# Three small jobs moved one quarter block later in TensorE's order: the second x half of a state-space group, the copy of the index keys, and the transpose of B in the second layer

## The chip, the cores and the metric

One core of one Trainium2 chip runs the whole program. Its engines are TensorE (PE in the profile: matmuls and transposes; PEld is its weight load), VectorE (DVE), ScalarE (ACT), GpSimd (POOL) and SyncE (SP, which issues nearly all DMAs). The metric is the device time of one execution in microseconds (us); the time of a kernel is the median of its runs.

## The reference, cut to what matters

Two layers work on 272 tokens (16 learned meta tokens and 256 inputs) of width 2048. All branches of a layer take their inputs from one projection, and their outputs go through one output projection:

```
h <- h + RMSNorm_post(W_out [ silu(gA)*PoolMix(vA) | SSD(xBC,z,dt) | silu(gC)*DSA(q,k,v) ])

SSD, for each of 4 groups of 8 heads:  xs, B, C = silu(conv4(xBC));  dt = softplus(.)
    cb = C B^T;   y = (cb * decay) (xs*dt)  +  C * state;   state = B^T (decay * xs*dt)
    y = y + D*xs;  y = RMSNorm_group(y * silu(z))
DSA:  ki = rope(index key);  score[q,s] = sum_h w_h relu(qi_h . ki[s]);  keep the 64 best s of each query
PoolMix:  windowed means of v, minus v, times a 256x256 matrix for each of 4 groups
```

Everything is fp32 in the reference. The second layer's first 16 tokens are needed only as inputs of the others, not as outputs.

## The kernel before

**Precision and weights.** Each weight matrix is cut into blocks of 256 columns, and a block into four quarters of 512 rows. A quarter is loaded in one DMA (`wr`). `split` then makes the two parts that the matmuls use, half a quarter at a time: ScalarE casts to fp32r (`wh`, line 211) and VectorE subtracts for the remainder (`wl`, line 219). `wh` has 10 buffers and `wl` 9, so both engines may run some four quarters ahead of TensorE. A product takes three matmuls (lines 244 to 246); a quarter block is 24 of them.

**Order.** The order of all engines is written out by the Python program, and each engine works strictly in the order in which its instructions are written. TensorE's main stream is the sequence of blocks: iq, k, v, q and ag, then for each group g of the state-space part xs(2g), xs(2g+1), BC(g), z(2g), z(2g+1), then pv and pg (pool), then the output projection. All work behind a block is a generator (`post_xs`, `post_BC`, `post_misc` and others). After each quarter block `tick()` resumes every generator once, in the order in which they were started; what a generator writes up to its next `yield n` stands between two quarter blocks, and `yield n` lets it sleep for n quarters. `yield from until(key)` sleeps in steps of one quarter until another generator has put `key` into `done`. Waits for data are then semaphores on the chip.

**Generators that the change and the prediction speak of.**
- `post_misc` turns the index keys and the dt columns. It writes the rope of the keys (`ikp`, finished on GpSimd, line 452), copies them (`ikh`, lines 478 and 489), multiplies them by a piece of the identity so that they also stand on partitions 0 to 63 (`pik`, line 486, on TensorE) and forms the remainders (`ikl`, line 490 on GpSimd, line 495 on VectorE). The key "ik" lets `post_iq` write the score matmuls `pq` (line 593), which read `ikh` and `ikl`. ScalarE then takes `s` from `pq` (line 598), and VectorE adds it into the scores (lines 605, 607). When all are in, VectorE picks the 64 best, and the attention heads (`pl`, line 674, which reads `qs`, line 763) begin.
- `post_xs(2g+j)` is half j of group g: evacuation, convolution on VectorE (line 802, six instructions), silu and the copy `xr` on ScalarE (lines 806, 826), transposes `px` on TensorE (lines 845, 847), `xdt` on VectorE (852, 855), a product on GpSimd (860), casts `xdd` on ScalarE (864, 865), remainders on VectorE (867, 868), and then the key `xdd{g}_{j}`. Half 0 of group g begins its convolution only after `until(y{g-1})`, that is when the last z half of the group before is written.
- `post_BC(g)` makes the convolution, silu and the copy `br` (886), sleeps `BY` quarters, and turns B (`pb`, 889, 890) and multiplies C by B (`pc`, 894); VectorE then writes `cbm` and the remainders of `bt` (899 to 904). It waits for `xdd{g}_0` and `xdd{g}_1`, sleeps one quarter and writes the state matmuls `pst` (913 to 917). Then it starts the four `decay` generators, whose last step sets `M{g}_{c}`.
- `post_z` waits for `M{g}_{c}`, writes the products of the group (`ssd_y`), and sets `y{g}` at the end of its second half; then it norms the group (`rsqrt_g`, eleven GpSimd instructions, lines 272 to 282) and writes the mix (1015, 562, 563).
- `post_pv(0)` waits for `y3`, makes the window sums on GpSimd (1040, 1042), and then `py_`, `pyh` and `pyl` (1045, 1049, 1052), and sets `ys0`. `pool_mm(0)` stands in TensorE's stream after the second quarter of the block pv1; it calls `tick()` in a loop until `ys0` is there, and then writes the matmuls `ppo` (1068 to 1070), which read `pyh` and `pyl`.

Of the kernel before, what the change touches and what calls it, by code (L numbers as in the profile page):

```python
# [10 lines left out]
F32 = mybir.dt.float32  # L11
F32R = mybir.dt.float32r
AF = mybir.ActivationFunctionType
OP = mybir.AluOpType
# [4 lines left out]
P = 128  # L19
# [71 lines left out]
BY = 1  # L91
# [11 lines left out]
def hybrid(ctx: ExitStack, tc: tile.TileContext, I, out, dbg=None, layers=2):  # L103
# [9 lines left out]
    sm = ctx.enter_context(tc.tile_pool(name="sm", bufs=2))  # L113
# [5 lines left out]
    V, A, G, TE = nc.vector, nc.scalar, nc.gpsimd, nc.tensor  # L119

    def pair(name):
        return pr.tile([P, 2, T], F32, name=name, tag="pair")

    def aux(name):
        return psa.tile([P, 512], F32, name=name, tag="a")

    def rep8(ap):

        return bc(ap[:, None, :], [ap.shape[0], 8, 16])

    def by8(ap):
        return ap.rearrange("p (e s) -> p e s", e=8)

    def dump(name, ap):
        if name in dbg:
            nc.gpsimd.dma_start(dbg[name], ap)

    def bc(ap, shape):
        return ap.to_broadcast(shape)
# [190 lines left out]
    ikh = const.tile([P, T], F32R, name="ikh")  # L330
    ikl = const.tile([P, T], F32R, name="ikl")
# [23 lines left out]
    def layer(L, hs):  # L355
# [11 lines left out]
        def until(key):  # L367
            while key not in done:
                yield 1
# [71 lines left out]
        def rope_v(dst, ps, nch, c0, idx):  # L441

            b = 2 if idx else 0
            n = T - c0
            t = pair("ropet")
            for i, p_ in enumerate(ps if isinstance(ps, list) else [ps[:, :nch]]):
                p_ = p_[:, None, :] if isinstance(ps, list) else p_
                m = p_.shape[1]
                V.stream_shuffle(t[:, i:i + m, c0:T], p_[:, :, c0:T], SHI if idx else SHQ)
                V.tensor_tensor(dst[:, i:i + m, c0:T], p_[:, :, c0:T], bc(rope[:, b:b + 1, c0:T], [P, m, n]), op=OP.mult)  # L450
            G.tensor_tensor(t[:, :nch, c0:T], t[:, :nch, c0:T], bc(rope[:, b + 1:b + 2, c0:T], [P, nch, n]), op=OP.mult)  # L451
            G.tensor_tensor(dst[:, :nch, c0:T], dst[:, :nch, c0:T], t[:, :nch, c0:T], op=OP.add)
# [16 lines left out]
        def post_misc(ps):  # L469
            yield from until("r")  # L470
            ps3 = ps[:, None, :]
            mt = pair("mt")
            V.tensor_tensor(mt[0:64, 0], ps[0:64, :T], r[0:64], op=OP.mult)
            V.tensor_copy(by8(mt[0:48, 1, 0:128]), rep8(mt[0:48, 0, 0:16]))
            ikp = pair("ikp")
            rope_v(ikp, ps3, 1, 0, True)
            yield 1
            A.copy(ikh[64:128], ikp[64:128, 0])
            ptr = aux("ptr")
            pv_ = ptr[:, 0:144].rearrange("p (b c) -> p b c", b=3)  # L480
            TE.transpose(pv_[:, 0], mt[0:48, 1, 0:128], ident[0:48, 0:48])
            for b in (1, 2):
                TE.transpose(pv_[:, b], mt[0:48, 0, TB[b][0]:TB[b][1]], ident[0:48, 0:48])  # L483

            pik = aux("pik")[0:64, 0:T]
            TE.matmul(pik, ident[:, 64:128], ikp[:, 0], start=True, stop=True)
            dx = sm.tile([P, 3, 48], F32, name="dx", tag="dx", bufs=1)
            yield 1
            A.copy(ikh[0:64], pik)
            G.tensor_tensor(ikl[64:128], ikp[64:128, 0], ikh[64:128].bitcast(F32), op=OP.subtract)  # L490
            V.tensor_copy(dx, pv_)
            V.tensor_scalar(iw, dx[:, 1:3, 32:48], 2.0 ** -5, None, op0=OP.mult)
            done.add("iw")
            yield 1
            V.tensor_tensor(ikl[0:64], pik, ikh[0:64].bitcast(F32), op=OP.subtract)
            done.add("ik")
            yield 1
            yield MY

            def st(name):  # L500
                return sm.tile([P, 3, 32], F32, name=name, tag=name, bufs=1)

            h_ = [wk.tile([P, n], F32, name="dtw", tag=tag) for n, tag in ((256, "bt"), (T, "cbm"))]
            n_, w_, z_, z2 = (t[:, o:o + 96].rearrange("p (b h) -> p b h", b=3) for t in h_ for o in (0, 96))
            x_, p_ = st("sx"), st("sp")
            ae = sm.tile([P, 1, 32], F32, name="ae", tag="ae", bufs=1)
            V.tensor_tensor(x_, dx[:, :, 0:32], bc(dtc[:, L, 0:1], [P, 3, 32]), op=OP.add)
            V.scalar_tensor_tensor(n_, x_, -1.0, x_, op0=OP.mult, op1=OP.min)
            A.activation(w_, n_, AF.Exp)
            A.activation(ae[:, 0], dtc[:, L, 1], AF.Exp)  # L510
            yield 1
            V.tensor_scalar(n_, w_, 2.0, None, op0=OP.add)
            V.reciprocal(z_, n_)
            V.tensor_tensor(z_, z_, w_, op=OP.mult)
            V.tensor_tensor(z2, z_, z_, op=OP.mult)
            V.tensor_scalar(p_, z2, 1.0 / 17, None, op0=OP.mult)
            for c in (15, 13, 11):
                V.scalar_tensor_tensor(p_, p_, 1.0 / c, z2, op0=OP.add, op1=OP.mult)
            yield 1
            for c in (9, 7, 5, 3):  # L520
                V.scalar_tensor_tensor(p_, p_, 1.0 / c, z2, op0=OP.add, op1=OP.mult)
            V.scalar_tensor_tensor(p_, p_, 1.0, z_, op0=OP.add, op1=OP.mult)
            V.tensor_scalar(n_, x_, 0.0, None, op0=OP.max)
            V.scalar_tensor_tensor(dt, p_, 2.0, n_, op0=OP.mult, op1=OP.add)
            da = st("sx")
            V.scalar_tensor_tensor(da, dt, -1.0, bc(ae, [P, 3, 32]), op0=OP.mult, op1=OP.mult)
            yield 1
            yield 1

            pcs = aux("pcs")  # L530
            TE.matmul(pcs[:, 0:32], tri8[0:16], da[0:16, 0], start=True, stop=True)
            for b in (1, 2):
                TE.matmul(pcs[:, 32 * b:32 * b + 32], tri, da[:, b], start=True, stop=True)
            for b in range(2):
                n = NB[b]
                TE.matmul(pcs[:, 96 + 32 * b:128 + 32 * b], ones[0:n, :], da[0:n, b], start=True, stop=True)
            pct = aux("pct")
            for b, (s0, s1) in enumerate(TB):
                n = s1 - s0
                TE.matmul(pct[0:32, s0:s1], da[0:n, b], tri[0:n, 0:n], start=True, stop=True)  # L540
            yield 1
            V.tensor_copy(cs, pcs[:, 0:96].rearrange("p (b h) -> p b h", b=3))
            V.tensor_tensor(wd, pcs[:, 96:160].rearrange("p (b h) -> p b h", b=2), cs[:, 0:2], op=OP.subtract)
            A.activation(wd, wd, AF.Exp)
            A.activation(dec, pcs[:, 128:160], AF.Exp)
            cst_ = pr.tile([32, T], F32, name="csT", tag="pair")
            V.tensor_copy(cst_, pct[0:32, :T])
            dump(f"dt{L}", dt.rearrange("p a b -> p (a b)"))
            dump(f"cs{L}", cst_)
            yield 1  # L550
            G.tensor_scalar(wd[:, 0], wd[:, 0], pa[:, MSK:MSK + 1], None, op0=OP.mult)
            A.dma_start(csd, cst_)
            done.add("cs")
# [254 lines left out]
        def post_xs(i, ps):  # L808
# [19 lines left out]
            if j == 0:  # L828
                yield from until("cs")
                if g == 0:  # L830
                    for a_ in range(4):
                        yield from until(f"mixA{a_}")
                s["xdt"] = wk.tile([P, 3, 8, 64], F32, name="xdt", tag="xdt")
                s["xdd"] = wk.tile([P, 3, 512], F32R, name="xdd", tag="xdd")
                s["csb"] = slots.tile([P, 8, T], F32, name="csb", tag=f"S{SP_[0]}")
                nc.sync.dma_start(s["csb"], csd[8 * g:8 * g + 8].rearrange("h t -> (h t)").partition_broadcast(P)
                                    .rearrange("p (h t) -> p h t", h=8))
                s["yg"] = wk.tile([P, 4, T], F32, name="yg", tag="yg")
            else:
                while "yg" not in s:  # L840
                    yield 1
            px = aux("px")
# [28 lines left out]
        def post_BC(g, ps):  # L871
# [12 lines left out]
            br = pair("br")[:, 0, 0:128]  # L884
            bT, cT = x[:, 0], x[:, 1]
            A.copy(by8(br), rep8(bT[:, 0:16]))
            yield BY
            pb = aux("pb")
            TE.transpose(pb[:, 0:P], br, ident)
            TE.transpose(pb[:, P:2 * P], bT[:, 16:144], ident)  # L890
# [202 lines left out]
        def lead_0():  # L1093
# [14 lines left out]
            for hh in range(8):  # L1108
# [10 lines left out]
                if hh == 3:  # L1119
                    early()  # L1120
            spawn(post_misc(pm))
            for b in range(NLEAD):
                spawn(post["iq"](b, lead[b]))

        def lead_1():
# [62 lines left out]
            for hh in range(8):  # L1188
# [8 lines left out]
                if hh > 4:  # L1197
                    tick()
            spawn(post_misc(pm))
            for i in range(2):  # L1200
                spawn(post_iq(i, e[i]))
# [312 lines left out]
```

## Time and profile before

| | us |
|---|---|
| median of three runs | 1584.16 |
| lowest, highest run | 1581.88, 1584.36 |
| the profiled execution: its own time | 1581.26 |
| the profiled execution: its span | 1579.5 |
| TensorE busy in the span | 1540.3 (98%) |
| VectorE, ScalarE, GpSimd busy | 1206.4 (76%), 884.6 (56%), 416.5 (26%) |
| mean granted TensorE clock | 0.997 |

The profiled execution ran 2.9 us faster than the median of the runs, and its time is 1.8 us more than its span. All rows are of this one execution. "Busy" counts the union of an engine's instructions. The number in brackets at the end of a timeline row is the idle time of that engine just before the instruction, with what ended it; a row with "xN" holds N instructions in a row, its second number being the time from the first one's start to the last one's end.

### The profile page before, as it was taken

The numbers are of one execution on the slowest core, as the hardware profiler recorded it, in microseconds if no ns is written. First come the engines' busy times: TensorE is split into PE (matmuls) and PEld (weight loads), VectorE is DVE, ScalarE is ACT, GpSimd is POOL, SyncE is SP. The second block draws the span as 40 slices with busy tenths as digits, with TensorE's granted clock in tenths as the row PEclk, the third lists the DMA queues.
The fourth block names the chain that finished last, engine by engine and source line by source line (L and its number), as shares of the span: only waits on it lengthen the run. The fifth ranks groups of instructions, "written<-read, shape, count | busy, mean of one in ns | idle before, by whom it ended". The sixth has DMA issues, their size and how long they took to land. (4 is left out here: it accounts for less than half of the span.)

```text
span 1579.5 us, 31128 instructions
## 1 busy us (share of the span) xinstructions
PE 1540.3 (98%) x11788; PEld 1475.4 (93%) x11788; DVE 1206.4 (76%) x2217; ACT 884.6 (56%) x1663; POOL 416.5 (26%) x416
## 2 busy tenths in 40 slices
PE   7999999999999999999998999999999999999997
PEld 6899999999999999999998999999999999988886
DVE  7899777798989776545588998787989888764554
ACT  6455566656667444444455555666676565444542
POOL 3823342233342421000103314322333324200000
PEclk9999999999999999999999999999999999999999
DMA  6545445454544465565536454454545455566652
GB/s 232 204 146 174 138 135 180 143 189 136 188 172 154 130 207 169 191 217 176 171 108 230 152 173 157 149 188 148 197 153 181 174 162 164 190 225 207 208 188 93
DMA packets 78310, 272.44 MB, mean 172 GB/s; under 512 B 8848, under 2 KB 11984, under 8 KB 77136
## 3 DMA queue, kind: packets, MB, share of 16 engines
q1 hardware_dynamic: 78064, 270.39, 51.5%
q8 instruction: 92, 1.51, 0.4%
q14 instruction: 58, 0.48, 0.1%
q10 hardware_dynamic: 96, 0.07, 0.0%
HBM read 266.03 MB, written 4.40 MB: 171 GB/s over the span
## 5 line engine op out<-in xcount | busy, mean ns | idle before, releaser
L219 DVE TENSOR_TENSOR wl<-wr,wh 128x512 fp32r<-128x512 f32 (+1 forms) x952 | 712.7, 773 | 270.0 <-PE go L246 70.5
L211 ACT CAST wh<-wr 128x512 fp32r<-128x512 f32 (+1 forms) x952 | 564.6, 615 | 430.2 <-PE go L245 91.7
L244 PE MATMUL g0xs<-u,wh 128*128 128x272 f32 x256 | 74.8, 292 | 0.0
L244 PE MATMUL g1xs<-u,wh 128*128 128x272 f32 x256 | 74.6, 291 | 0.0
L244 PE MATMUL g0z<-u,wh 128*128 128x272 f32 x256 | 74.5, 291 | 0.0
L246 PE MATMUL go<-mixS,wl 128*128 128x272 f32 x256 | 74.1, 290 | 0.0
L246 PE MATMUL g0xs<-u,wl 128*128 128x272 f32 x256 | 74.1, 290 | 0.0
L246 PE MATMUL g0z<-u,wl 128*128 128x272 f32 x256 | 74.1, 290 | 0.0
L246 PE MATMUL g1xs<-u,wl 128*128 128x272 f32 x256 | 74.1, 289 | 0.0
L244 PE MATMUL go<-mixS,wh 128*128 128x272 f32 x256 | 74.0, 289 | 0.0
L245 PE MATMUL g1xs<-u,wh 128*128 128x272 f32 x256 | 73.7, 288 | 0.0
L245 PE MATMUL g0xs<-u,wh 128*128 128x272 f32 x256 | 73.7, 288 | 0.0
L245 PE MATMUL g0z<-u,wh 128*128 128x272 f32 x256 | 73.6, 288 | 0.0
L245 PE MATMUL go<-mixS,wh 128*128 128x272 f32 x256 | 73.6, 288 | 0.0
L244 PE MATMUL g1z<-u,wh 128*128 128x256 f32 x256 | 72.7, 284 | 0.0
L451 POOL TENSOR_TENSOR ropet<-ropet,rope 128x512 f32<-128x512 f32 (+2 forms) x20 | 33.2, 1661 | 147.7 <-PE ptr L483 66.1
L246 PE MATMUL g1z<-u,wl 128*128 128x256 f32 x256 | 71.7, 280 | 0.0
L245 PE MATMUL g1z<-u,wh 128*128 128x256 f32 x256 | 71.6, 280 | 0.0
L948 POOL TENSOR_TENSOR M<-M,cbm 128x512 f32<-128x512 f32 x32 | 45.9, 1434 | 93.4 <-ACT M L941 93.4
L802 DVE SCALAR_TENSOR_TENSOR xs<-xpad,par,xs 128x272 f32<-128x272 f32 x96 | 62.1, 712 | 0.0
L1262 POOL TENSOR_TENSOR acc<-acc,osq 128x544 f32<-128x544 f32 x6 | 8.2, 1370 | 168.8 <-ACT osq L1248 168.8
L266 PE MATMUL got<-wh,mixS 128*128 128x512 f32 x128 | 50.8, 397 | 0.0
(531 smaller groups left out, 5523.9 us busy)
## 6 DMA issues: line engine op xcount, KB each, us to landing
wr<-wi SPq DMA_DIRECT2D x334, 512.0 KB, 3.3
wr<-wo SPq DMA_DIRECT2D x128, 512.0 KB, 3.4
csb<-csd SPq DMA_DIRECT2D x8, 1088.0 KB, 8.4
x<-xT SPq DMA_DIRECT2D x8, 272.0 KB, 5.0
res<-xT SPq DMA_DIRECT2D x4, 544.0 KB, 6.0
h1d<-o SPq DMA_DIRECT2D x4, 544.0 KB, 7.7
wr<-plw SPq DMA_DIRECT2D x8, 256.0 KB, 2.6
hx<-h1d SPq DMA_DIRECT2D x8, 256.0 KB, 3.7
```

Source lines behind the costliest of these rows:

```text
L211: A.copy(hi, r[:, 2 * h:2 * h + 2])
L219: V.tensor_tensor(lo, r[:, 2 * h:2 * h + 2], his[i].bitcast(F32), op=OP.subtract)
L244: TE.matmul(o, w_h, u[:, 0, k, t1:T], start=first and k == 0, stop=False)
L245: TE.matmul(o, w_h, u[:, 1, k, t1:T], start=False, stop=False)
L246: TE.matmul(o, w_l, u[:, 0, k, t1:T], start=False, stop=last and k == 3)
L266: TE.matmul(o, m_h, hi, start=first, stop=False)
L451: G.tensor_tensor(t[:, :nch, c0:T], t[:, :nch, c0:T], bc(rope[:, b + 1:b + 2, c0:T], [P, nch, n]), op=OP.mult)
L802: V.scalar_tensor_tensor(dst[:, c], x[:, c, 13 + j:13 + j + T], w[:, j:j + 1], dst[:, c], op0=OP.mult, op1=OP.add)
L948: G.tensor_tensor(M[:, hh, 16:], M[:, hh, 16:], bc(cbm[:, None, 16:], [P, 2, 256]), op=OP.mult)
L1262: G.tensor_tensor(acc[:, :, t0:], acc[:, :, t0:], s[:, :, t0:], op=OP.add)
```

## The change

No instruction is added and none is taken out. In `post_misc`, in both layers, the copy of the keys, the matmul `pik` and what reads it are written one quarter later than before, while the three transposes of the dt columns stay; the key "ik" is set at the same quarter as before. In `post_xs`, the second half of a group sleeps one quarter more before its transposes `px`. In `post_BC`, B is turned two quarters after its copy in the second layer (L is 1 there), and one quarter after it in the first, as before.

```diff
@@ post_misc
             yield 1
-            A.copy(ikh[64:128], ikp[64:128, 0])
             ptr = aux("ptr")
             pv_ = ptr[:, 0:144].rearrange("p (b c) -> p b c", b=3)
             TE.transpose(pv_[:, 0], mt[0:48, 1, 0:128], ident[0:48, 0:48])
             for b in (1, 2):
                 TE.transpose(pv_[:, b], mt[0:48, 0, TB[b][0]:TB[b][1]], ident[0:48, 0:48])
+            dx = sm.tile([P, 3, 48], F32, name="dx", tag="dx", bufs=1)
+            yield 1
+            A.copy(ikh[64:128], ikp[64:128, 0])
 
             pik = aux("pik")[0:64, 0:T]
             TE.matmul(pik, ident[:, 64:128], ikp[:, 0], start=True, stop=True)
-            dx = sm.tile([P, 3, 48], F32, name="dx", tag="dx", bufs=1)
-            yield 1
-            A.copy(ikh[0:64], pik)
-            G.tensor_tensor(ikl[64:128], ikp[64:128, 0], ikh[64:128].bitcast(F32), op=OP.subtract)
             V.tensor_copy(dx, pv_)
             V.tensor_scalar(iw, dx[:, 1:3, 32:48], 2.0 ** -5, None, op0=OP.mult)
             done.add("iw")
             yield 1
+            A.copy(ikh[0:64], pik)
+            G.tensor_tensor(ikl[64:128], ikp[64:128, 0], ikh[64:128].bitcast(F32), op=OP.subtract)
             V.tensor_tensor(ikl[0:64], pik, ikh[0:64].bitcast(F32), op=OP.subtract)
             done.add("ik")
             yield 1
@@ post_xs
             else:
+                yield 1
                 while "yg" not in s:
                     yield 1
             px = aux("px")
@@ post_BC
             A.copy(by8(br), rep8(bT[:, 0:16]))
-            yield BY
+            yield BY + L
             pb = aux("pb")
```

## Rows read from the trace of the kernel before

**Rows 1.** The page: the span, and TensorE's busy time with its share and the number of its instructions.

```profile
span 1579.5 us, 31128 instructions
PE 1540.3 (98%) x11788; PEld 1475.4 (93%) x11788; DVE 1206.4 (76%) x2217; ACT 884.6 (56%) x1663; POOL 416.5 (26%) x416
```

**Rows 2.** Who waited for whom, TensorE's waits over the whole span: total us, how often, the longest.

```profile
PE px L845 <- ACT xr L826: 6.0, 6, 1.1
PE g0iq L246 <- DVE wl L219: 5.4, 3, 2.8
...
PE pik L486 <- POOL ikp L452: 4.0, 2, 2.2
```

**Rows 3.** Busy time by windows of 3.40 us: busy us and number of instructions of PE, PEld, DVE, ACT and POOL, then the granted TensorE clock, then the DMA share and GB/s.

```profile
20.00:23.40 3.40, 3.39 (x28) 3.40 (x29) 3.12 (x6) 3.40 (x9) 2.17 (x1) 1.00 0.44 129
53.00:56.40 3.40, 3.40 (x16) 3.12 (x15) 3.40 (x4) 2.56 (x5) 3.32 (x3) 0.50 0.31 84
855.20:858.60 3.40, 3.40 (x14) 2.60 (x14) 3.40 (x7) 2.16 (x5) 3.40 (x1) 0.50 0.41 122
```

**Rows 4.** TensorE's timeline around the index keys and the scores, first in the first layer, then in the second.

```profile
52.59 0.77 PE L486 MATMUL pik<-ikp,cst 128*64 128x272 f32 x2 [1.82 <-POOL ikp L452]
...
66.86 0.33 PE L593 MATMUL pq<-ikh,iqh 64*128 64x144 f32 x1 [0.33 <-DVE ikl L495]
75.84 0.33 PE L593 MATMUL pq<-ikh,iqh 64*128 64x144 f32 x1 [0.34 <-ACT s L598]
77.40 0.33 PE L593 MATMUL pq<-ikh,iqh 64*128 64x144 f32 x1 [1.23 <-ACT s L598]
...
855.03 1.08 PE L486 MATMUL pik<-ikp,cst 128*64 128x272 f32 x2 [2.16 <-POOL ikp L452]
...
868.74 0.33 PE L593 MATMUL pq<-ikh,iqh 64*128 64x144 f32 x2
...
878.36 0.33 PE L593 MATMUL pq<-ikh,iqh 64*128 64x144 f32 x1 [0.48 <-ACT s L598]
...
936.31 0.39 PE L674 MATMUL pl<-ks,qs 128*128 128x272 f32 x1 [1.63 <-DVE qs L763]
```

**Rows 5.** VectorE's timeline up to the remainder of the keys, first in the first layer, then in the second.

```profile
53.29 8.49 DVE L219 TENSOR_TENSOR wl<-wr,wh 128x512 fp32r<-128x512 f32 x6
...
66.39 0.42 DVE L495 TENSOR_TENSOR ikl<-pik,ikh 64x272 fp32r<-64x272 f32 x1
...
865.96 1.98 DVE L219 TENSOR_TENSOR wl<-wr,wh 128x512 fp32r<-128x512 f32 x2 [4.99 <-ACT wh L211]
867.87 0.42 DVE L495 TENSOR_TENSOR ikl<-pik,ikh 64x272 fp32r<-64x272 f32 x1
```

**Rows 6.** The timeline in group 3 of the first layer, from the convolution of half 0 to the transpose of B: VectorE's rows, then ScalarE's, then TensorE's.

```profile
457.81 3.60 DVE L802 SCALAR_TENSOR_TENSOR xs<-xpad,par,xs 128x272 f32<-128x272 f32 x6
...
468.50 0.87 DVE L219 TENSOR_TENSOR wl<-wr,wh 128x512 fp32r<-128x512 f32 x1 [0.32 <-PE g0BC L246]
469.30 4.80 DVE L802 SCALAR_TENSOR_TENSOR xs<-xpad,par,xs 128x272 f32<-128x272 f32 x6
...
479.19 1.29 DVE L563 TENSOR_TENSOR mixS<-yg,mixS 128x1088 fp32r<-128x1088 f32 x1 [0.20 <-ACT mixS L562]
...
485.81 2.55 DVE L802 SCALAR_TENSOR_TENSOR BC<-xpad,par,BC 128x272 f32<-128x272 f32 x6
...
489.08 0.30 ACT L886 COPY br<-BC 128x128 f32<-128x128 f32 x1
...
476.97 0.33 PE L845 MATMUL px<-cst,xr 128*128 128x128 f32 x1 [1.02 <-ACT xr L826]
...
489.77 0.27 PE L889 MATMUL pb<-cst,br 128*128 128x128 f32 x1
```

**Rows 7.** The same in group 2 of the second layer, up to the state matmuls: VectorE's rows, then TensorE's.

```profile
1172.87 3.53 DVE L802 SCALAR_TENSOR_TENSOR xs<-xpad,par,xs 128x272 f32<-128x272 f32 x6
...
1183.51 0.74 DVE L219 TENSOR_TENSOR wl<-wr,wh 128x512 fp32r<-128x512 f32 x1 [0.42 <-PE g1BC L246]
...
1193.85 1.22 DVE L563 TENSOR_TENSOR mixS<-yg,mixS 128x1024 fp32r<-128x1024 f32 x1 [0.21 <-ACT mixS L562]
...
1200.45 2.55 DVE L802 SCALAR_TENSOR_TENSOR BC<-xpad,par,BC 128x272 f32<-128x272 f32 x6
...
1206.99 0.29 DVE L904 TENSOR_TENSOR bt<-pb,bt 128x128 fp32r<-128x128 f32 x1
...
1207.80 1.28 DVE L219 TENSOR_TENSOR wl<-wr,wh 128x512 fp32r<-128x512 f32 x2
...
1204.07 0.33 PE L889 MATMUL pb<-cst,br 128*128 128x128 f32 x1 [0.20 <-ACT br L886]
...
1207.63 0.40 PE L913 MATMUL pst<-xdd,bt 128*128 128x512 f32 x1
```

**Rows 8.** The timeline at the first pool matmuls, in the first layer and in the second: VectorE's last remainder, and TensorE's first matmul that reads it.

```profile
536.87 1.29 DVE L1052 TENSOR_TENSOR pyl<-py__7047,pyh 128x544 fp32r<-128x544 f32 x1
...
540.44 0.28 PE L1069 MATMUL ppo<-pyl,wh 128*128 128x272 f32 x1
...
1316.60 1.26 DVE L1052 TENSOR_TENSOR pyl<-py__17106,pyh 128x544 fp32r<-128x544 f32 x1
...
1319.75 0.28 PE L1069 MATMUL ppo<-pyl,wh 128*128 128x256 f32 x1
```

## The prediction

> **What bounds the kernel now.** I read the page first, then the list of waits, then windows of the span for the granted clock, then the timelines of the places that the diff touches. On the page the reader is to see that TensorE is busy for 1540.3 of 1579.5 us [rows 1]: it can give back 39 us at most, and only where it waits. The list of waits says where the change aims: six waits of `px` for the copy `xr`, 6.0 us in all, and two of `pik` for the keys on GpSimd, 4.0 us [rows 2]; I leave the 5.4 us of weights alone, which the diff does not touch. The windows are to show a second price: just after each `pik` wait TensorE runs at a granted clock of 0.50 (the 1.2 GHz level), with 16 and 14 matmuls begun in 3.4 us, where 28 begin at 1.00 (2.4 GHz) right after a 2.8 us wait of another kind that ends near 20 us [rows 2, 3]. So not every wait costs clock; each of these two did, and half speed for 3.4 us is 1.7 us of work lost. The timelines then say what is late next, because no instruction is added or removed: every term is a wait that moves. A quarter block lasts about 3.0 us here (24 matmuls, at 28 to a window of 3.4 us [rows 3], are 2.9; where transposes stand between them it is 3.0).
>
> **The keys (`post_misc`).** Removed: 1.82 + 2.16 = 3.98 us of wait [rows 4], and 2 x 1.7 = 3.4 us of lost clock, together 7.4 us. Now `pik` comes a quarter later than its input. What is late next is `pq`, which reads `ikl`. VectorE gets to `ikl` by its own work: in the first layer it runs from 53.29 to 66.81 (66.39 + 0.42) behind a row of `wl`, in the second it waits 4.99 us for ScalarE's `wh` and ends at 868.29 [rows 5]. Neither waits for TensorE, and the key "ik" stays at its quarter, so `ikl` lands when it did. TensorE would now come to `pq` 1.82 + 1.7 = 3.5 us early in the first layer, where it already waits 0.33 us at 66.86, and 3.9 us early in the second, where it has 0.45 us to spare (868.74 against 868.29) [rows 4, 5]. It waits there instead. I take it that a wait this long, 3.4 to 3.9 us, again brings the lower clock, for 1.7 us. In the first layer the later waits of 0.34 and 1.23 us on `s` swallow that; in the second 1.7 - 0.45 = 1.25 us is left, of which 0.48 us goes at 878.36 and the rest in the 1.63 us wait for `qs` at 936.31 [rows 4]. Net 0. Bounds: -7.4 if `ikl` were early too, +3.4 if both drops were paid and nothing swallowed them.
>
> **The x halves (`post_xs`).** The extra `yield` of half 1 carries `px`, `xdt`, `xdd`, the remainders, `pst`, the decays, `M`, the products `ssd_y` and so `y{g}` along. The copy `xr` is then a quarter old and the wait for it goes: 1.02 us a time in the first layer [rows 6], 6.0 us over six [rows 2]; group 0 of each layer has no such wait, and I price it at 0. But half 0 of the next group writes its convolution only after `y{g}`, so it starts a quarter later, while half 1's convolution and that of B and C keep their places. Three convolutions are squeezed. In group 3 of the first layer VectorE goes from 457.81 to 488.36 (485.81 + 2.55) with idle times of 0.32 and 0.20 us only; in group 2 of the second from 1172.87 to 1203.00 with 0.42 and 0.21 [rows 6, 7]. That stretch begins 3.0 us later, less the idle 0.5 to 0.6, less the two `wl` of a quarter that now stand ahead of it (1.28 us for two [rows 7]): the convolution of B and C ends 3.0 - 0.52 - 1.28 = 1.2 us later in the first layer and 2.95 - 0.63 - 1.28 = 1.0 in the second. The bound above is 2.4: the six instructions of line 802 took 2.55 to 3.60 us in two places and 4.80 in a third [rows 6], and a second slow one would cost 1.2 more. The bound below is 0, if the `wl` that stay behind the convolutions can fill all of it. I take the middle, since the trace has two of three convolutions at the faster price.
>
> The slow convolution, at 469.30, took 4.80 us where the others took 2.55 and 3.60 [rows 6]; the norm of the group before, eleven GpSimd instructions, is written near it. The Trainium skill says why that may be, in "GPSIMD Engine Reference", section "8. Key points": GpSimd and VectorE share their SBUF interfaces, and VectorE instructions with two SBUF inputs contend. The durations agree with it but do not prove it; if it held for all that the move pushes under the norm, it would speak against the change and give the rival below with 2.4 us.
>
> *First layer, B not moved.* `br` is ready at 489.08 + 0.30 + 1.2 = 490.6. TensorE, without its 1.02 us wait, comes to `pb` at 489.77 - 1.02 = 488.75 [rows 6]. It waits 1.8 us there in place of 1.02 at `px`: +0.8 for each of groups 1 to 3, +2.4 together; bounds -3.1 (`br` ready before TensorE comes, the wait simply gone) and +6 (2.4 late: 3.05 - 1.02 = 2.0 each).
>
> **B in the second layer (`BY + L`).** `pb` comes a quarter later too, so its wait (0.20 [rows 7]) goes with the wait of `px` there, (6.0 - 3 x 1.02) / 3 = 0.98 [rows 2, 6]: -1.2 a group. What is late next is `pst`, which reads `bt`. Its last remainder ended at 1207.28 (1206.99 + 0.29) [rows 7]; with VectorE 1.0 later and about 1.8 us of other work (two `wl`, 1.28, and an evacuation) now ahead of it, that is 1210.1. TensorE's `pst`, at 1207.63 before, moves by a quarter less the gain, 2.95 - 1.2 = 1.75, to 1209.4. It waits 0.7 to 0.8: -0.4 a group, -1.2 for three; bounds -3.6 and +3.
>
> **Clock at the new waits.** Three waits of 1.8 us at `pb` in the first layer are as long as the 1.82 of `pik` that lost 1.7 us [rows 4], and shorter than the 2.8 that lost nothing [rows 2, 3]. I take one of three: +1.7, with ends 0 and 5.1.
>
> **The pool.** `y3` is a quarter later, so `post_pv(0)` is too, and `pool_mm(0)` calls `tick()` once more before it writes `ppo`. `pyl` ended at 538.16 and 1317.86, its reader began at 540.44 and 1319.75, so 2.3 and 1.9 us were to spare [rows 8]. A quarter more leaves TensorE 3.0 - 2.3 = 0.7 and 2.9 - 1.9 = 1.0 short: +1.7; ends 0 and 5.9 (the whole quarter twice). The DMAs of these generators move with their steps, in the same order on the same queues and in the same number; the only one near a use, the broadcast of half 0, has some ten quarters in hand. I price them at 0.
>
> **Sum.** 0 + 2.4 - 1.2 + 1.7 + 1.7 = +4.6 us on an execution of 1581.26: 1585.9. That execution lies 2.9 us under the median of 1584.16, so the forecast is 1588.8 us, 0.29% slower. Less than 0.2% either way, 3.2 us, is about what a measurement of this kernel can tell from no change.
>
> **Rivals.**
> - *Faster: the convolutions are not squeezed.* If VectorE takes the quarter out of its lead over TensorE, `br` is not late. At the old moment, 489.38, it still holds TensorE for 0.63 of the 1.02 us won (it comes at 488.75), which leaves -0.4 a group, -1.2 in the first layer; the second keeps its -3.6; the pool takes 1.7: -3.1. If `br` follows TensorE and comes 0.63 earlier, the first layer keeps 3.1 and the sum is -5.0. So 1579 to 1581, say 1580. For it: ten `wh` and nine `wl` buffers are a lead of four quarters. Against it: in the whole stretch VectorE idles for 0.5 us [rows 6]. It decides from a lateness below 0.4 us, where the first layer turns from loss to gain. Chance 0.27.
> - *The keys pay.* If `ikl` comes as early as TensorE, 7.4 us stay won: 1588.8 - 7.4 = 1581.4. Against it: VectorE's 13.5 us without a wait for TensorE [rows 5]. Chance 0.08.
> - *The squeeze is dear.* Lateness 2.4, and each `pb` wait of 3 us loses clock: 3 x 2.0 + 3 x 1.0 + 3 x 1.7 + 1.7 = +15.8, about 1600 us. For it: the 4.80 us row [rows 6]. Chance 0.12.
> - *The wait only changes its name.* `pb` takes over just what `px` gave, the pool's slack holds: 1584, within 2. Chance 0.12.
>
> The forecast itself has 0.41, with a range of its own from 1586 to 1592. The range for all, 1579 to 1600, cuts off some of the first rival and half of the third, less than 0.2. Faster by over 0.2%, below 1581: 0.20 of the first rival and 0.04 of the second make 0.24. Within: 0.07 and 0.04 of the same two, the 0.12, and a fifth of the forecast (below 1587.3), 0.09, make 0.32. Slower: 0.32 and 0.12 make 0.44.
>
> **What the profile after would show.** `px` and `pik` gone from TensorE's list of waits; `pq` there for `ikl` with two waits of 3.4 to 3.9 us, and a clock of 0.50 behind them instead of at 53 and 855; `pb` waiting for `br` some 1.8 us three times in the first layer; `pst` waiting under 1 us for `bt` in the second; `ppo` waiting 0.7 and 1.0 for `pyl`. It is wrong if `ikl` moves ahead by more than a microsecond, if the convolution of B and C ends where it did, or if the new waits at `pb` are not there.

## The result, and the profile after

The changed kernel took 1592.15 us (median of six runs, 1587.78 to 1595.02), the kernel before 1583.7 us in six runs. The ratio is 1.0056 with a 95% interval of 1.0042 to 1.007: slower by 8.5 us by the medians, 6.7 to 11 us by the interval. The forecast was 1588.8, slower, with 1579 to 1600 as its range.

The page of the profiled execution after: the span, and the busy time of the engines, to be held against [rows 1].

```profile
span 1590.2 us, 31151 instructions
PE 1545.1 (97%) x11788; PEld 1480.4 (93%) x11788; DVE 1208.8 (76%) x2217; ACT 884.3 (56%) x1663; POOL 414.7 (26%) x416
```

The span grew by 10.7 us, TensorE's busy time by 4.8 of them with the same 11788 matmuls, so part of the loss is not waiting but slower matmuls. TensorE's waits after (total us, how often, longest), which answer to [rows 2]:

```profile
PE pb L890 <- ACT br L887: 6.8, 3, 2.3
...
PE pq L593 <- DVE ikl L495: 3.7, 2, 3.0
PE pst L914 <- DVE bt L904: 3.1, 3, 1.0
PE ppo L1070 <- DVE pyl L1053: 2.4, 2, 1.3
...
PE pq L593 <- ACT ikh L493: 2.2, 1, 2.2
```

`px` and `pik`, 10 us of waits before, are gone from the list. In their places stand `pb` for `br` in the first layer, `pq` for the keys, `pst` for `bt` in the second layer and `ppo` for `pyl`: 18.2 us where the same groups had 0.9 before (`pb` 0.6, `pq` for `ikl` 0.3). Windows of the changed kernel (busy us and instructions of PE, PEld, DVE, ACT and POOL, then granted clock, DMA share, GB/s), each taken behind one of these waits. The first and last stand behind `pq`; the other three, of 5.40 us, begin right behind the waits of `pb`:

```profile
70.40:73.80 3.40, 3.40 (x17) 3.40 (x18) 2.42 (x5) 0.62 (x2) 3.40 (x1) 0.50 0.66 210
350.50:355.90 5.40, 5.40 (x31) 5.14 (x32) 4.68 (x11) 3.56 (x8) 0.00 (x0) 0.68 0.63 197
424.20:429.60 5.40, 5.40 (x31) 5.25 (x32) 4.97 (x12) 3.52 (x8) 0.00 (x0) 0.68 0.68 200
497.90:503.30 5.40, 5.40 (x44) 5.25 (x45) 5.17 (x13) 4.12 (x9) 0.00 (x0) 1.00 0.63 202
879.70:883.10 3.40, 3.40 (x18) 3.40 (x18) 3.40 (x3) 0.57 (x3) 3.28 (x2) 0.50 0.21 54
```

The clock is 0.50 (1.2 GHz) behind both waits of `pq`, as forecast. Behind the three waits of `pb`, of 2.23, 2.27 and 2.28 us, it is lower after two and not after the third: 0.68 on average over 5.40 us means 1.7 us of work lost each time (5.40 x 0.32), and 31 matmuls are begun where the third window has 44.

**Where the time went, stretch by stretch.** The weight matmuls are the same and in the same order in all kernels, so the start of the n-th one can be compared with the start of the same one before. The table gives how much the profiled execution of a kernel fell behind that of before within each stretch, in us (negative: gained); the first column, up to 47.5 us, lies ahead of every edit but that of e11.

| kernel | start | keys, 1st layer | groups 1 to 3, 1st | pool, 1st | keys, 2nd layer | groups 1 to 3, 2nd | pool, 2nd | all |
|---|---|---|---|---|---|---|---|---|
| after | +2.1 | -0.6 | +6.6 | +1.2 | +0.2 | -0.2 | +1.6 | +10.8 |
| e1 keys alone | +2.6 | -0.3 | 0.0 | 0.0 | 0.0 | 0.0 | 0.0 | +2.2 |
| e2 x half alone | +0.5 | -0.5 | +5.1 | +1.2 | -0.2 | +9.1 | +1.6 | +16.7 |
| e3 x half, B in both | +2.4 | +0.6 | -2.8 | +1.2 | -0.2 | -0.2 | +1.6 | +2.5 |
| e4 early key | +1.1 | -0.6 | +13.4 | +0.5 | -0.1 | +6.6 | 0.0 | +20.7 |
| e6 half 0 late | +0.6 | 0.0 | -0.8 | 0.0 | +1.0 | +0.3 | 0.0 | +0.9 |
| e7 x half, B, pool | +2.4 | +0.7 | -2.8 | -0.2 | +1.6 | -0.2 | 0.0 | +1.4 |
| e8 the same with the keys | +1.6 | -0.5 | -2.8 | -0.2 | -0.1 | -0.2 | 0.0 | -2.2 |
| e9 half 0 and norm late | +1.3 | -0.5 | +0.9 | -0.3 | 0.0 | +3.5 | 0.0 | +5.0 |
| e10 norm late | +1.6 | +0.7 | +9.9 | -0.3 | +0.3 | +9.4 | 0.0 | +21.6 |
| e11 short norm | -0.2 | -2.7 | -3.8 | +0.8 | -0.1 | -4.8 | +1.2 | -9.3 |
| e12 half 0 late, B | +2.6 | -0.5 | -0.6 | +1.2 | +0.5 | +2.2 | +1.6 | +6.9 |

What is left to the sum lies in the long stretches between, and moves by 0.3 us at most. The first column says how to read the others: up to 47.5 us nothing was edited (except in e11, whose shorter norm also stands there), and yet single executions of the others differ from that of before by up to 2.6 us, with waits for `wl` and a lower clock behind them that fall differently from one to the next. Without it the changed kernel is 8.7 us behind, which is what the medians say. Three quarters of that lies in groups 1 to 3 of the first layer; the pool takes 2.8, and the keys and the second layer's groups together give back 0.6.

### The profile page after: what moved, and what is told of

Read it like the earlier page. It is cut to its first block, busy times and chain, and to the rows that moved or that the text cites. A ratio compares the mean times of both kernels' runs of the same rounds, so it can differ in the third digit from the quotient of the medians.

```text
span 1590.2 us, 31151 instructions
## 1 busy us (share of the span) xinstructions
PE 1545.1 (97%) x11788; PEld 1480.4 (93%) x11788; DVE 1208.8 (76%) x2217; ACT 884.3 (56%) x1663; POOL 414.7 (26%) x416
```

## The experiments

**e1: the keys alone.** The edit of `post_misc` in both layers, the rest as before.

> Only the edit of the index keys, in both layers; everything else as before. Theory (the wait of pik is only moved, because ikl hangs on VectorE's own work and not on TensorE): pik waits for nothing, pq waits for ikl 3.0 to 3.3 us in the first layer and about 3 us in the second, the clock is 0.50 behind these waits instead of behind pik, and the time is that of before within 2 us, 1582 to 1586. Rival, the keys pay: 4 us of wait and 3.4 us of clock stay won, 1576. Rival, the keys are where the loss comes from: 5 us or more above before, 1589.

Measured: 1582.39 us against 1583.33, ratio 0.9997 (0.9988 to 1.0005). The waits of TensorE:

```profile
PE px L845 <- ACT xr L826: 6.0, 6, 1.1
...
PE pq L593 <- DVE ikl L495: 3.7, 2, 3.0
...
PE pq L593 <- ACT ikh L493: 2.2, 1, 2.2
```

`pq` waits 3.00 us in the first layer and 3.17 in the second, where the new place of the copy `ikh` shows as the longest part (2.18, then 0.69 for `ikl` and 0.30 for `iql`). Both stretches end within 0.3 us of before. The keys are no part of the loss and no gain. The kernels that keep the keys of before show why: in e2, e3, e6, e7, e9, e10 and e12 `pik` waits about 1.4 us in the first layer, with no lower clock behind it, and `pq` then waits 1.8 us for `ikl`, where the execution of before, with 1.82 us and the lower clock at `pik`, waits 0.33.

**e5: the keys with a later key "ik".** The idea was to let the score matmuls come a quarter later too.

```diff
+            yield 1
             done.add("ik")
-            yield 1
```

> The edit of the index keys as in the change, and the key that releases the score matmuls one quarter later still, in both layers; everything else as before. Theory: ikl lands as before, and TensorE comes to pq about when it does, so that the wait of 3 us and the lower clock behind it go in both layers. The first layer keeps the 3.5 us; in the second qs hangs on VectorE's own row, pl waits for it some 4 us instead of 1.6, and nothing or at most a microsecond is won: 3 us under before, 1580. Rival: the score chain is late by the same quarter in the first layer too, later waits (s, qs) take it all, and the time is that of before within 1 us.

Measured: 1582.82 us, ratio 0.9997 (0.9988 to 1.0005), and `pq` waits 3.09 us. The edit did nothing at all: every engine has the instructions of e1 in the same order, since "ik" is not the last of the keys that `post_iq` waits for. The question of the expectation was not tested; the run stands as a second measurement of e1.

**e2: the x half alone.** The `yield 1` in half 1, in both layers, with B turned one quarter after its copy in both.

> Only the extra quarter of half 1 in both layers; keys as before, and B is turned one quarter after its copy in both layers. Theory (half 0 of the next group starts later, the convolution of B and C ends 1 to 1.5 us late): the first layer's groups lose the 6.6 us that the profile after shows there, with three waits of pb of 2.2 us; the second layer's lose likewise, with pb waits near 2 us, in place of px 0.95 and pb 0.2: 0.8 us a group, 2.4 us, and up to 1.7 us more for each wait that costs clock; the pool 2.9 us. Sum +12 to +17, 1596 to 1601. Rival, the squeeze is one of the first layer alone: +9.5, 1593.

Measured: 1599.72 us, against 1583.33, ratio 1.0108 (1.0093 to 1.0124), 16.4 us.

```profile
PE pb L890 <- ACT br L887: 15.5, 6, 2.9
```

Six waits of `pb` in place of three: 2.2 to 2.3 us in the first layer, 2.84, 2.94 and 2.95 in the second. The second layer loses 3.0 us a group. Its waits account for 2.9 - 1.15 = 1.75 of it (before, `px` 0.95 and `pb` 0.2 stood there); behind each of the three the matmuls run at the lower clock for a while. So the mechanism is not one of the first layer alone: the edit `BY + L` shelters the second.

**e3: the x half, with B two quarters after its copy in both layers.**

```diff
-            yield BY
+            yield BY + 1
```

> The extra quarter of half 1, and B turned two quarters after its copy in both layers; keys as before. Theory: what the first layer loses hangs on the place of pb alone, so that with pb a quarter later it does as the second layer does in the profile after: no wait of pb, a wait of pst for bt of about 1 us a group, no clock lost there, 0 against before; the pool's 2.9 us stay: 1586 to 1588. Rival, VectorE's lateness itself is what costs: the wait moves whole to pst, 2 us or more a group with a lower clock, and the time stays 6 us or more above before, 1590 or more.

Measured: 1582.56 us, ratio 0.9997 (0.9988 to 1.0006); the forecast for it was 1586 to 1588.

```profile
PE pst L914 <- DVE bt L904: 3.1, 3, 1.0
PE ppo L1070 <- DVE pyl L1053: 2.4, 2, 1.3
```

With `pb` a quarter later, the first layer waits neither there nor at `pst` and gains 0.94 us a group, where the changed kernel loses 2.2. All three waits of `pst` are in the second layer, 1.0 us each, and eat up the gain there. The pool's 2.8 us take back what the first layer gives. The place of `pb` in the first layer alone decides between +6.6 and -2.8 us, the keys being free.

**e4: an early key for half 0 and the pool.** The changed kernel, but half 0 of the next group and the first pool block wait for a key that is set a quarter before `y{g}`.

```diff
                 ssd_y(g, c, yo)
+                if c == 3:
+                    done.add(f"e{g}")
...
-                    yield from until(f"y{g - 1}")
+                    yield from until(f"e{g - 1}")
...
-                yield from until("y3")
+                yield from until("e3")
```

> The whole change, but half 0 of the next group and the first pool block are released by a key that is set a quarter before y (after the last products of the group are written), so that they start where they started before. Theory: br is on time, pb in the first layer waits 0.6 us in place of the 2.3 of the changed kernel, with no clock lost, pst in the second layer waits 0.2 us or less, ppo waits for nothing: 1.2 us and 3.6 us better than before, 1579. Rival, the lateness comes from the products, remainders and norm that also moved a quarter and now stand ahead of the convolution of B and C: pb still waits 1.5 us or more, and only the pool's 2.9 us come back, 1589.

Measured: 1602.78 us, ratio 1.0122 (1.0108 to 1.0136). Neither theory had this: `pb` waits 3.15 us in the first layer, and `px` waits again. ScalarE's timeline in group 3 of the first layer of this kernel:

```profile
486.67 0.41 ACT L865 CAST xdd<-xr 128x256 fp32r<-128x256 f32 x1 [5.34 <-POOL xr L861]
487.69 0.41 ACT L866 CAST xdd<-xr 128x256 fp32r<-128x256 f32 x1 [0.61 <-POOL xr L861]
488.00 0.65 ACT L806 ACTIVATE xs<-xs 128x544 f32<-128x544 f32 x1
488.69 0.49 ACT L826 COPY xr<-xs 128x128 f32<-128x128 f32 x2
```

The cast `xdd` of half 0 waits 5.34 us for a product on GpSimd, and behind it in ScalarE's order stand silu and `xr` of half 1. The same four rows of the kernel before:

```profile
474.60 0.41 ACT L864 CAST xdd<-xr 128x256 fp32r<-128x256 f32 x1 [2.65 <-POOL xr L860]
475.62 0.41 ACT L865 CAST xdd<-xr 128x256 fp32r<-128x256 f32 x1 [0.61 <-POOL xr L860]
475.93 0.65 ACT L806 ACTIVATE xs<-xs 128x544 f32<-128x544 f32 x1
476.62 0.50 ACT L826 COPY xr<-xs 128x128 f32<-128x128 f32 x2
```

and what GpSimd does ahead of that product, before:

```profile
472.96 0.84 POOL L282 TENSOR_TENSOR ysq<-ysq 128x272 f32<-128x272 f32 x1
473.76 1.83 POOL L860 TENSOR_TENSOR xr<-xdt,wd 128x256 f32<-128x256 f32 x2
```

The product comes right behind line 282, the last of the norm. So the wait of `px` that the change aims at may never have been one for the convolution, which had ended at 474.10 [rows 6], but for the norm of the group before. e6, e9 and e10 test that, and which of the moved things makes B late.

**e6: half 0 late, nothing else.**

```diff
                     yield from until(f"y{g - 1}")
+                    yield 1
```

> Before, with one edit: half 0 of groups 1 to 3 begins its convolution one quarter later; px of half 1, the products, the norm, B, the pool and the keys stay where they were. Theory (it is half 0's later start that makes the convolution of B and C late): px of half 1 waits 1 us more than before, about 2 us, pb 0.5 us more, 1.5 us a group in the first layer and 1 to 1.5 in the second, about 8 us in all and up to 1.7 us more for each wait that costs clock: 1591 to 1596. Rival (the products, remainders and norm that the change moves along are what is late): px and pb wait as before, 1583.

Measured: 1582.97 us, ratio 0.9999 (0.999 to 1.0008). The theory fell: half 0 late is free.

```profile
PE pb L890 <- ACT br L887: 3.2, 6, 0.9
PE px L846 <- ACT xr L827: 0.9, 4, 0.3
```

`px` now waits 0.9 us in all (6.0 before), although nothing about `px` was edited: with half 0 a quarter later, its casts stand behind silu and `xr` of half 1 and no longer ahead of them. And the convolution of B and C is on time; VectorE's rows in group 3 of the first layer, where this execution is 0.3 us behind that of before:

```profile
470.79 4.48 DVE L802 SCALAR_TENSOR_TENSOR xs<-xpad,par,xs 128x272 f32<-128x272 f32 x6
475.19 1.28 DVE L219 TENSOR_TENSOR wl<-wr,wh 128x512 fp32r<-128x512 f32 x2
...
485.89 2.56 DVE L802 SCALAR_TENSOR_TENSOR BC<-xpad,par,BC 128x272 f32<-128x272 f32 x6
```

Half 1's convolution starts 1.2 us later than in [rows 6] (470.79 - 0.3 against 469.30), as the squeeze says, and yet BC's starts at the old time. What makes it good is the `wl` in between: 1.28 us for two, where the kernel before has

```profile
474.02 2.12 DVE L219 TENSOR_TENSOR wl<-wr,wh 128x512 fp32r<-128x512 f32 x2
```

with GpSimd at the end of the norm and at the product beside it.

**e9: half 0 and the norm late.** e6 with `PNY` 3 in place of 2, which moves the norm and the mix (the group's output written for the projection) one quarter on.

> Before, with half 0 of groups 1 to 3 one quarter later (as in the run that did this alone) and the norm and mix of each group one quarter later too; px of half 1, the products, B, the pool and the keys stay. Theory (half 0 late costs nothing alone because VectorE then works less beside GpSimd; with the norm late as well GpSimd runs beside VectorE's wl and convolutions again): the convolution of B and C ends 1.5 us late in both layers, pb waits about 1.9 us in the first layer (0.2 with half 0 late alone) and 2.3 us in the second (0.85), +9 us and up to 1.5 us more for each wait that costs clock: 1591 to 1597. Rival (the lateness comes from px and the products that the change also moves): pb as with half 0 late alone, 1583.

Measured: 1587.31 us, ratio 1.0027 (1.0018 to 1.0037).

```profile
PE pb L890 <- ACT br L887: 10.7, 6, 2.2
```

`pb` waits 1.36 us in the first layer (0.22 in e6) and 2.2 in the second (0.85). The expectation had the direction and 1.1 to 1.4 of the 1.5 us of lateness, but its total of 9 us left out that the waits of `px`, 1 us a group, go at the same time; 4.5 us came.

**e10: the norm late alone.** The kernel before with `PNY` 3.

> Before, with the norm and mix of each group one quarter later and nothing else. Theory (the wait of px in the kernel before is not one for the convolution: ScalarE's casts xdd of half 0 wait for a product that stands behind the norm in GpSimd's row, and silu and xr of half 1 stand behind these casts): px waits 3.5 to 4 us in place of 1.0 in the first layer and some 3 in the second, 2 to 3 us a group more, 12 to 18 us in all and clock beside: 1595 to 1605. Rival (px waits for the convolution): px as before, the pn and mix steps only move, 1583 to 1585.

Measured: 1602.26 us, ratio 1.012 (1.0103 to 1.0137). TensorE's and ScalarE's waits:

```profile
PE px L845 <- ACT xr L826: 19.2, 6, 3.2
...
ACT xdd L864 <- POOL xr L860: 28.6, 6, 4.9
```

`px` waits 3.2 us instead of 1.0 when only the norm and the mix behind it move, and the cast `xdd` waits up to 4.9 us for GpSimd. That settles what `px` waited for in the kernel before: the norm, by way of the product on GpSimd and the cast on ScalarE.

**e11: the changed kernel with a short norm.** Of the norm's eleven GpSimd instructions one scale and one multiplication stay, nine are left out (the first layer's input norm calls the same function, which is why the column of the first keys gains 2.7 us in this row).

> The changed kernel with the norm's inverse root left out: two of its eleven GpSimd instructions stay, so the norm is wrong in value and short in time. Theory (the wait of pb comes from VectorE working beside the norm): without the norm the convolution of B and C ends 1.5 us earlier or more, pb waits 0.5 us or less in the first layer and pst under 0.3 us in the second, the pool's wait stays: 9 to 11 us under the changed kernel, 1581 to 1583. Rival (the order on VectorE alone makes it late): pb still waits 1.2 us or more, 1588 or more.

Measured: 1574.18 us, ratio 0.9942 (0.9927 to 0.9957). No wait of `px`, `pb` or `pst` is left, and each group is 1.3 to 1.6 us faster than before. The expectation had 1581 to 1583: the direction held, but the kernel is 18 us under the changed one in place of 9 to 11, 2 us of it at the first layer's keys, behind the shorter input norm. VectorE in group 3 of the first layer, first the changed kernel (its weight matmuls there start 6.9 us later than before, by the table's measure), then e11, whose line 793 is 802 of the others:

```profile
475.38 1.13 DVE L219 TENSOR_TENSOR wl<-wr,wh 128x512 fp32r<-128x512 f32 x1 [0.42 <-PE g0BC L246]
476.43 0.41 DVE L853 TENSOR_TENSOR xdt<-px,dt 128x256 f32<-128x256 f32 x1
...
477.43 4.66 DVE L802 SCALAR_TENSOR_TENSOR xs<-xpad,par,xs 128x272 f32<-128x272 f32 x6
482.00 4.13 DVE L219 TENSOR_TENSOR wl<-wr,wh 128x512 fp32r<-128x512 f32 x4
...
492.85 0.42 DVE L853 TENSOR_TENSOR xdt<-px,dt 128x256 f32<-128x256 f32 x1
493.84 2.91 DVE L802 SCALAR_TENSOR_TENSOR BC<-xpad,par,BC 128x272 f32<-128x272 f32 x6
```

```profile
465.20 2.91 DVE L793 SCALAR_TENSOR_TENSOR xs<-xpad,par,xs 128x272 f32<-128x272 f32 x6
468.03 2.55 DVE L219 TENSOR_TENSOR wl<-wr,wh 128x512 fp32r<-128x512 f32 x4
...
478.29 2.91 DVE L793 SCALAR_TENSOR_TENSOR BC<-xpad,par,BC 128x272 f32<-128x272 f32 x6
```

The same ten VectorE instructions, six of a convolution and four `wl`, take 4.66 + 4.13 = 8.79 us beside the norm and 5.46 without it: 3.3 us a group, more than the 1.5 us by which B is late. That is not the difference between the two kernels, since the kernel before pays part of it as well (4.80 us for the convolution [rows 6] and 2.12 for two `wl`). And e11 takes more away than the change added: the product and the casts behind the norm come earlier too. What the norm's place does with all of its work left in is read from e6 against e9.

**e7 and e8: the parts put together.** e7 is e3 with the remainder `pyl` of the first pool block written in the step of the cast `pyh`; e8 has the keys' edit as well, and is thus the changed kernel with `pb` a quarter later in the first layer too and the pool's `pyl` a step earlier; its later key "ik" is that of e5, which changed nothing.

```diff
             A.copy(yh, y)
-            yield 1
+            if i:
+                yield 1
```

> The extra quarter of half 1, B two quarters after its copy in both layers, keys as before, and for the first pool block the remainder pyl written in the same step as the cast pyh, so that its key is set at the quarter of before. Theory: the parts add; the 1.2 and 1.6 us of ppo go, the first layer keeps the 0.95 us a group: 2.8 us under before, 1580.5. Rival: VectorE waits for pyh at the new place and holds up the wl behind it, so that the pool's loss only changes its name: 1583.

> The kernel with the pool's remainder a step earlier, and the keys' edit with the score matmuls one quarter later in both layers. Theory: the parts add, 2.8 us and 3 us: 1577 to 1578, 0.35% under before. Rival: the keys give nothing, 1580 to 1581.

Measured: e7 1581.25 us, ratio 0.9989 (0.998 to 0.9997); e8 1579.17 us, ratio 0.9979 (0.997 to 0.9988), against 1582.84 for before. The waits of `ppo` are gone in both and the first layer keeps its 2.8 us. e8 is faster than both kernels. The expectation's 3 us for the keys have no ground (e5); by the stretches e8's keys cost nothing (-0.5 and -0.1), and e7's execution lost 0.7 and 1.6 in the same stretches with the keys of before. Whether that difference between e7 and e8 is one of the keys or of single executions, their intervals don't settle.

**e12: half 0 late, and B two quarters after its copy.** A shorter way to the same aim, after e6: no edit of `px`.

> Before, with half 0 of groups 1 to 3 one quarter later and B turned two quarters after its copy in both layers; px of half 1, the norm, the pool and the keys stay where they were. Theory (half 0 late takes the casts xdd out of the way of xr, costs VectorE nothing while the norm stays in place, and a pb a quarter later takes its wait away): px waits 0.3 us or less, pb for nothing, pst for 0.3 us or less, ppo as before; 0.9 us a group won in both layers, 5 us in all: 1577 to 1579. Rival (bt is late for pst by the moved quarter, as in the changed kernel): pst waits 1 us in the second layer and the gain there is gone, 1580 to 1581.

Measured: 1586.9 us, ratio 1.0024 (1.0015 to 1.0033). Both forecasts, 1577 to 1579 and 1580 to 1581, missed.

```profile
PE pst L914 <- DVE bt L904: 4.1, 6, 1.0
...
PE ppo L1070 <- DVE pyl L1053: 2.4, 2, 1.3
```

The pool's loss is back though nothing of the pool or of `px` was touched: a later `pb` makes `pst`, the decays and `y{g}` a quarter late, and with `y{g}` the norm and the pool follow, and half 0 a second quarter on top. Every edit that moves `y{g}` brings the norm along.

## Why the prediction was right, and where its steps were not

**The keys, 0: right.** `pq` waits 3.04 us in the first layer and 3.34 in the second (2.20 + 0.68 + 0.46; forecast 3.4 to 3.9), and the clock falls behind them: -0.6 and +0.2 us, and 0.9997 for the edit alone in e1. The waits on `s`, 2.1 us before, are gone as forecast; the wait on `qs` swallowed nothing, it is 1.6 us in both kernels.

**The first layer's groups: right in sign, too small.** Forecast +2.4 for the waits and +1.7 for the clock, measured +6.6. `pb` waits 2.23 to 2.28 us and not 1.8, which makes 3 x (2.26 - 1.06) = 3.6; the lower clock behind two of the three waits, where one was forecast, costs 2 x 1.7 = 3.4 us. That is 7.0, of which 0.4 comes back in the stretch at places that were not followed up. The price of a drop was right, the number of drops was a guess: the same three waits are followed by one drop in e2. The lateness of the convolution of B and C was forecast as 1.2 us; it ends at 496.75, less 6.87 us by which the weight matmuls run behind there 489.88, against 488.36: 1.5 us (the 6.87 us are those of 467 to 474 us, ahead of `px` of half 1).

**What fell short in this step is its reason.** It took the 1.2 us from a later half 0 squeezing three convolutions. e6 moves half 0 alone, and B is on time: half 1's convolution starts 1.2 us late, and VectorE makes it good between there and B, because its `wl` then fall behind the norm (1.28 us for two in e6, 2.12 before). In the changed kernel the norm moves the same quarter, four `wl` take 4.13 us beside it, and nothing is made good; e9, with half 0 and the norm late and all else in place, brings back 1.1 to 1.4 us of it, and e11, with the norm short, brings B in time. The third rival named GpSimd's company as something that could make the squeeze dearer; it decides whether the squeeze costs anything. So part of the hit is luck: 1.2 us came close to 1.5 because the change happens to move the norm along with half 0, and the prediction did not count on that. The Trainium skill's rule in "GPSIMD Engine Reference", section "8. Key points", that GpSimd and VectorE instructions with two SBUF inputs contend, is in line with all of these rows; how much, the rows alone say: 8.79 against 5.46 us.

**The wait that the change removes was misread too.** The prediction took `px` to wait for a convolution that had just ended, because the list of waits names `xr` [rows 2, 6]. The list names only the last step. ScalarE's order ahead of `xr` shows the cast `xdd` of the other half, and that waits for GpSimd. This did not change the sum, as the wait goes either way; it would have shown that half 0's later start alone takes 5.1 of the 6.0 us away.

**The second layer's groups: -1.2 forecast, -0.2 measured.** `pst` waits for `bt` as said, 1.03 us and not 0.7 to 0.8 in each group. It waits for the first remainder of `bt` (line 904 of the changed kernel, 903 before); the prediction counted from the last one, 0.3 us later, so its own sum should have given less. e2 shows what the edit of B is worth there: without it the same stretch loses 9.1 us.

**The pool: +1.7 forecast, +2.8 measured.** `ppo` waits 1.13 and 1.31 us, and not 0.7 and 1.0. The place and the cause (a call of `tick()` more) are borne out by e7, where the step taken out again takes both waits away.

**The sum.** +4.6 forecast, +8.5 by the medians, +8.7 by the table. Of the difference the first layer's groups make 2.5 us (0.46 us more at each `pb` and a second drop of the clock), the pool 1.1 and the second layer's groups 1.0, and the keys give 0.4 back. All but the keys lean the same way, so the sign came out, with half of the size.

## What to carry to other kernels

A list of waits names the last link; before a wait is priced, follow the waiting engine's own order back past the releaser, since an instruction of another job may stand ahead of it and wait for a third engine. When a step is moved, list every generator that hangs on its keys, and ask beside which work each of them will now run: here the norm on GpSimd came along unseen, and beside it B came 1.5 us late, more than the 1.06 us of wait that was removed. A wait of 1 us taken from a place that nobody else depends on is worth no more than the slack of the next reader, so move the reader too (`pb` in the first layer) or leave both.

## What the runs showed of the hardware that was not expected

VectorE's instructions with two inputs in SBUF slow down by a factor of 1.6 while GpSimd works through a row of tensor operations (4.66 and 4.13 us against 2.91 and 2.55). The multiplication `xdt`, which takes one input from PSUM (`px`), does not: 0.41 us beside the norm at 476.43, 0.42 away from it at 492.85. And the granted clock behind a wait near 2.3 us is not settled by its length: of the changed kernel's three `pb` waits of 2.23 to 2.28 us two were followed by 0.68 over 5.40 us and one by 1.00. In e2, with three waits of the same lengths in the first layer, slow matmuls follow one of them; in e5 full clock follows a wait of 3.09 us at `pq`; in e10 they follow five of six `px` waits of 3.2 us; behind the `pst` waits of 1.0 us and the `px` waits of 1.1 us there are none. Ahead of 47.5 us, where no kernel but e11 was edited, executions differ by up to 2.6 us with the `wl` waits and the clock behind them.
